# The last loads of a softmax over row dot products: eleven transfers in place of nine, the last one half a row

## The chip, the cores and the metric

The kernel runs on one core of a Trainium2 chip. The metric is the device time of one launch in microseconds (us): 320.58 us is the median of three runs of the kernel before, from 320.44 to 320.85 us.

## What is computed

Inputs x and y have 8 batches of 4096 rows of 512 float32 numbers. Only the diagonal of the product x·yᵀ is needed, that is one dot product of row n of x with row n of y, and then a softmax over the 4096 dots of each batch.

```
gram = np.matmul(x, y.transpose(0, 2, 1))
diag = np.diagonal(gram, axis1=1, axis2=2)
diag = diag - diag.max(axis=-1, keepdims=True)
exp = np.exp(diag)
return (exp / exp.sum(axis=-1, keepdims=True)).astype(np.float32)
```

The inputs are 134.2 MB and the output 0.13 MB. Each number is read once, multiplied once and added once.

## The kernel before

**Tiling.** The 8 batches are two sets of four. Within a set the 128 partitions hold 4 batches by 32 stretches of 128 rows, so each partition owns 128 rows of a set. They are taken in steps of R = 32 rows; two sets of four steps make eight steps, t = 0 to 7. A step of x, or of y, is a block of 128 partitions by 16384 float32 numbers, 8.39 MB. x goes by turns into two tiles, `xs0` (even t) and `xs1` (odd t); y always into the one tile `ys`. Dot r of a step lands in a column of `diag0` (first set) or `diag1` (second set).

**Order.** The schedule is written out by hand: each engine runs its instructions in the order of the text. All loads and the stores of the first set are issued by the queue of SyncE (SP); the final store is issued by ScalarE.

**Steps 0 to 5** (lines 124 to 135): VectorE multiplies x by y in place (line 72, in two instructions, the second from a copy `side` that ScalarE makes of the last 6 rows of y, so that `ys` is free sooner), then sums each row (line 75); ScalarE sums two rows (line 80). The load of the next y waits until VectorE and ScalarE have read the tile `ys`.

**Step 6** (lines 137 to 147) does the same with ScalarE summing 30 rows.

**Step 7, the last** (lines 150 to 162), comes in nine transfers: x 15 rows, y 17, x 8, y 10, x 6, y 3, x 2, y 2, x 1. After each transfer `dots` (line 82) issues, for every row of which both halves are there, one fused instruction on VectorE (line 85): product and sum over 512 numbers, the sum going to the row's column of `diag1`. The first y transfer reuses the part of `ys` that step 6 has read first, and the second (y 10) waits for the last product of step 6.

**Completion semaphores.** SP's transfers use eight completion semaphores by turns, so the transfer that takes a semaphore again is issued only once the transfer eight places earlier has landed. In step 7 the x 15 rows have number 6, y 17 number 7, x 8 number 0, y 10 number 1, and so on to x 1 with number 6.

**The stores of the first set** (lines 167 and 168) stand in SP's text behind all loads: eight pieces of 16 partitions, each 8 KB. They take the semaphores from number 7 on: the second waits for x 8, the third for y 10, and the eighth for x 1, the last load.

**The end** (lines 169 and 170): the row maxima of the last 16 dots and of two maxima taken before (`mxp`, line 99), the maximum over the 32 partitions of a batch (`nmx`, line 93), the exponentials with their sum on ScalarE (line 106), the sum over the partitions (`sum`), the reciprocal (`rc`), the scaling (line 113), and the store from ScalarE (line 170). Each of these waits for the one before.

**Addresses.** In each partition `xs0` begins at byte 16512, `xs1` at 82048 and `ys` at 147584; each of the three is 128 bytes past a multiple of 512.

Of the kernel before, what the change touches and what calls it, by code (L numbers as in the profile page):

```python
# [1 line left out]

# [5 lines left out]


@with_exitstack
def kernel(
    ctx: ExitStack,
    tc: tile.TileContext,
    x: bass.AP,
    y: bass.AP,
    out: bass.AP,
):
    nc = tc.nc
    ctx.enter_context(tc.manual_schedule())  # L20
    f32 = mybir.dt.float32
    Alu = mybir.AluOpType
    Act = mybir.ActivationFunctionType
    X = mybir.AxisListType.X
    B, N, D = x.shape
    P = nc.NUM_PARTITIONS
    G = 32
    Q = P // G
    C = N // G
    R = 32  # L30
    H = R // 2
    K = 6
    W = 2
    F = H + 1
    L = 9
    S = B // Q * (C // R)


    xv = x.rearrange("(s b) (j c) d -> s (b j) c d", b=Q, j=G)
    yv = y.rearrange("(s b) (j c) d -> s (b j) c d", b=Q, j=G)  # L40
    ov = out.rearrange("(s b) (j c) -> s (b j) c", b=Q, j=G)

    big = ctx.enter_context(tc.tile_pool(name="big", bufs=1))
    small = ctx.enter_context(tc.tile_pool(name="small", bufs=1))


    xs = [big.tile([P, R, D], f32, name=f"xs{i}") for i in range(2)]
    ys = big.tile([P, R, D], f32, name="ys")
    side = big.tile([P, K, D], f32, name="side")

    diag = [small.tile([P, C + 2 * i], f32, name=f"diag{i}") for i in range(B // Q)]
    res = [small.tile([P, C], f32, name=f"res{i}") for i in range(B // Q)]

    def columns(t, r0, n):
        c0 = t % (C // R) * R + r0
        return slice(c0, c0 + n)

    def rows(t, r0, n):
        return xs[t % 2][:, r0 : r0 + n, :]

    def dots_of(t, r0, n):
        return diag[t * R // C][:, columns(t, r0, n)]

    def load_x(t, r0, n):
        nc.sync.dma_start(out=rows(t, r0, n), in_=xv[t * R // C, :, columns(t, r0, n), :])  # L65

    def load_y(t, r0, n):
        nc.sync.dma_start(out=ys[:, r0 : r0 + n, :], in_=yv[t * R // C, :, columns(t, r0, n), :])  # L68

    def products(t, r0, n, yt):  # L70
        xt = rows(t, r0, n)
        nc.vector.tensor_tensor(out=xt, in0=xt, in1=yt, op=Alu.mult)  # L72

    def sums(t, r0, n):
        nc.vector.tensor_reduce(out=dots_of(t, r0, n), in_=rows(t, r0, n), axis=X, op=Alu.add)  # L75

    def sums_act(t, r0, n):
        for r in range(r0, r0 + n):
            row = xs[t % 2][:, r, :]
            nc.scalar.activation(out=row, in_=row, func=Act.Copy, accum_out=dots_of(t, r, 1))  # L80

    def dots(t, r0, n):
        for r in range(r0, r0 + n):
            xt = xs[t % 2][:, r, :]
            nc.vector.scalar_tensor_tensor(  # L85
                out=xt, in0=xt, scalar=1.0, in1=ys[:, r, :], op0=Alu.mult, op1=Alu.mult,
                accum_out=dots_of(t, r, 1),
            )

    def over_quadrant(name, column, op, negate=False):  # L90

        got = small.tile([P, 1], f32, name=name)
        nc.vector.tensor_reduce(  # L93
            out=got, in_=column.to_broadcast([P, G]), axis=X, op=op, negate=negate, apply_transpose=True
        )
        return got

    def largest(out, d):
        nc.vector.tensor_reduce(out=out, in_=d, axis=X, op=Alu.max)  # L99

    def exps(i, d):
        mxp = small.tile([P, 1], f32, name=f"mxp{i}")
        largest(mxp, d)
        nmx = over_quadrant(f"nmx{i}", mxp, Alu.max, negate=True)
        sump = small.tile([P, 1], f32, name=f"sump{i}")
        nc.scalar.activation(out=res[i], in_=diag[i][:, :C], func=Act.Exp, bias=nmx, scale=1.0, accum_out=sump)  # L106
        return sump

    def normalize(i, sump):
        total = over_quadrant(f"sum{i}", sump, Alu.add)  # L110
        rc = small.tile([P, 1], f32, name=f"rc{i}")
        nc.vector.reciprocal(out=rc, in_=total)  # L112
        nc.vector.tensor_single_scalar(out=res[i], in_=res[i], scalar=rc, op=Alu.mult)  # L113

    nc.scalar.preload_act_table(Act.Exp)  # L117
    nc.vector.addr_align(128, offset=0, max_nops=0)
    nc.scalar.addr_align(128, offset=0, max_nops=0)

    nc.sync.drain()  # L121
    nc.sync.drain()  # L122

    for t in range(S - 2):
        load_x(t, 0, R)
        load_y(t, 0, R)
        nc.scalar.activation(out=side, in_=ys[:, R - K :, :], func=Act.Copy)  # L127
        if t == C // R:
            normalize(0, sump)
        products(t, 0, R - K, ys[:, : R - K, :])  # L130
        products(t, R - K, K, side)
        sums(t, 0, R - W)
        sums_act(t, R - W, W)
        if t == C // R - 1:
            sump = exps(0, diag[0])

    t = S - 2
    load_x(t, 0, R)
    load_y(t, 0, R)
    spare = rows(t + 1, R - L, L)  # L140
    nc.scalar.activation(out=spare, in_=ys[:, F - L : F, :], func=Act.Copy)  # L141
    products(t, 0, F - L, ys[:, : F - L, :])
    products(t, F - L, L, spare)
    products(t, F, R - F, ys[:, F:, :])
    sums(t, R - W, W)
    sums_act(t, 0, R - W)
    largest(diag[1][:, C + 1 :], diag[1][:, : C - 2 * R])


    t += 1  # L150
    upto = {load_x: 0, load_y: 0}
    done = 0
    for load, n in (
        (load_x, H - 1), (load_y, F), (load_x, 8), (load_y, 10), (load_x, 6), (load_y, 3), (load_x, 2), (load_y, 2), (load_x, 1)
    ):
        load(t, upto[load], n)
        upto[load] += n
        both = min(upto.values())
        dots(t, done, both - done)
        done = both  # L160
        if done == F:
            largest(diag[1][:, C : C + 1], diag[1][:, C - 2 * R : C - R + H])

    met = small.tile([P, C - R], f32, name="met")
    nc.scalar.activation(out=met, in_=diag[1][:, : C - R], func=Act.Copy)  # L165

    for p in range(0, P, H):
        nc.sync.dma_start(out=ov[0, p : p + H, :], in_=res[0][p : p + H, :])
    normalize(1, exps(1, diag[1][:, C - R + H :]))
    nc.scalar.dma_start(out=ov[1], in_=res[1])  # L170


# [1 line left out]
_INS = ['x', 'y']  # L174
_OUTS = [((8, 4096), 'float32')]


# [23 lines left out]
```

## Time and profile before

| | |
|---|---|
| median of three runs | 320.58 us (320.44 to 320.85) |
| span of the profiled execution, first to last instruction | 318.6 us |
| around that span (median less span) | about 2.0 us |
| read from memory | 134.22 MB, 422 GB/s over the span |
| VectorE busy | 241.6 us, 76% |
| ScalarE busy | 49.8 us, 16% |

The page of the profile gives, for one execution, the busy time of each engine (DVE is VectorE, ACT ScalarE, POOL GpSimd, SP SyncE), the share of the DMA engines in 40 slices, the chain of work that ended last, the costliest groups of instructions, and the DMA issues with the time from issue to landing. Finer views give that chain and the instructions in order of time: start, duration, engine, line, operation. A name such as SPq or DVEq is the engine's instruction queue. A transfer's landing is its issue time plus its time to landing; several transfers in one queue overlap, so a time to landing of 19 us is mostly waiting behind earlier bytes. No time of its own is listed for the profiled execution beyond the span.

### The profile page before, as it was taken

Reading aid. Unit: us, or ns where it says so; the run is one execution under the profiler, and the core shown is the slowest. Engines: PE = TensorE matmul, PEld = TensorE weight load, DVE = VectorE, ACT = ScalarE, POOL = GpSimd, SP = SyncE. Lnnn points to the kernel's source line nnn. Section 1 sums busy time; section 2 is a strip of 40 time slices with the busy share of each in tenths; the row PEclk is TensorE's granted clock in tenths of the full one; section 3 lists DMA queues with packets and bytes.
Section 4 is the critical chain, followed back from the end, with each engine's and each line's share of the span. In section 5 each row is a group of like instructions: output and inputs, shape, how many; then the busy total and the mean of one; then the engine's idle time right before and its main releaser. Section 6 shows DMA issues by size and latency. Waiting matters only on the chain.

```text
span 318.6 us, 315 instructions
## 1 busy us (share of the span) xinstructions
DVE 241.6 (76%) x98; ACT 49.8 (16%) x97; POOL 0.2 (0%) x4
## 2 busy tenths in 40 slices
DVE  0000069995899939999399994999939998599996
ACT  1000030100301003010120103001030100596700
POOL 0000000000000000000000000000000000000000
DMA  9999999999999999999999999999999999999993
GB/s 389 403 395 486 436 395 436 486 395 395 494 428 395 469 453 395 395 510 411 395 477 444 395 444 477 395 395 494 428 395 469 453 395 403 432 443 413 427 411 120
DMA packets 3714, 134.37 MB, mean 422 GB/s; under 512 B 512, under 2 KB 768, under 8 KB 1280
## 3 DMA queue, kind: packets, MB, share of 16 engines
q1 hardware_dynamic: 3568, 134.29, 97.8%
q10 hardware_dynamic: 144, 0.07, 0.1%
q14 instruction: 2, 0.02, 0.0%
HBM read 134.22 MB, written 0.13 MB: 422 GB/s over the span
## 4 chain that ended last, share of the span: by engine, by line
DMA 65%; DVE 33%; SPq 1%; issue 0%; ACT 0%; DVEq 0%
DMA ys<-in_y_dram 65%; DVE xs L72 32%; DVE xs L85 0%; SPq L65 0%; SPq L68 0%; DVE res L113 0%; DVE sum L93 0%; DVE nmx L93 0%; ACT res L106 0%; DVE mxp L99 0%; DVE rc L112 0%; DVEq L72 0%; SPq L122 0%; SPq L121 0%
## 5 line engine op out<-in xcount | busy, mean ns | idle before, releaser
L72 DVE TENSOR_TENSOR xs<-xs,ys 128x13312 f32<-128x13312 f32 (+2 forms) x8 | 96.7, 12091 | 71.7 <-DMA ys<-in_y_dram 71.7
L75 DVE TENSOR_REDUCE diag<-xs 128x30 f32<-128x15360 f32 (+1 forms) x7 | 98.1, 14019 | 0.2
L80 ACT ACTIVATE xs<-xs 128x512 f32<-128x512 f32 x42 | 25.9, 617 | 90.4 <-DVE xs L72 90.4
L127 ACT ACTIVATE side<-ys 128x3072 f32<-128x3072 f32 x6 | 16.6, 2763 | 124.3 <-DMA ys<-in_y_dram 124.3
L85 DVE SCALAR_TENSOR_TENSOR xs<-xs,ys 128x512 f32<-128x512 f32 x32 | 19.9, 686 | 1.1 <-DMA ys<-in_y_dram 1.0
L72 DVE TENSOR_TENSOR xs<-xs,side 128x3072 f32<-128x3072 f32 x6 | 20.1, 3350 | 0.0
L80 ACT ACTIVATION_READ_ACCUMULATOR xs<-xs 128x1 f32 x42 | 7.9, 187 | 0.0
L141 ACT ACTIVATE xs<-ys 128x4608 f32<-128x4608 f32 x1 | 4.0, 4043 | 20.0 <-DMA ys<-in_y_dram 20.0
L106 ACT ACTIVATE res<-diag,nmx 128x128 f32<-128x128 f32 x2 | 0.8, 401 | 30.1 <-DVE nmx L93 30.1
L72 DVE TENSOR_TENSOR xs<-xs,xs 128x4608 f32<-128x4608 f32 x1 | 5.0, 4951 | 0.0
L85 DVE DVE_READ_ACCUMULATOR xs<-xs,ys 128x1 f32 x32 | 2.6, 81 | 0.0
L117 ACT ACT_TABLE_LOAD x1 | 1.3, 1283 | 0.7 <-PEq L185 0.7
L93 DVE TRANSPOSE_TENSOR_REDUCE sum<-sump 128x1 f32<-128x32 f32 x2 | 0.4, 211 | 1.2 <-ACT res L106 1.2
L113 DVE TENSOR_SCALAR res<-res,rc 128x128 f32<-128x128 f32 x2 | 0.6, 286 | 0.1
L99 DVE TENSOR_REDUCE mxp<-diag 128x1 f32<-128x128 f32 (+1 forms) x2 | 0.5, 228 | 0.1
L93 DVE TRANSPOSE_TENSOR_REDUCE nmx<-mxp 128x1 f32<-128x32 f32 x2 | 0.4, 211 | 0.1
L99 DVE TENSOR_REDUCE diag<-diag 128x1 f32<-128x64 f32 (+1 forms) x2 | 0.4, 202 | 0.0
L112 DVE RECIPROCAL rc<-sum 128x1 f32<-128x1 f32 x2 | 0.3, 164 | 0.1
L106 ACT ACTIVATION_READ_ACCUMULATOR res<-diag,nmx 128x1 f32 x2 | 0.4, 186 | 0.0
L165 ACT ACTIVATE met<-diag 128x96 f32<-128x96 f32 x1 | 0.3, 282 | 0.0
L185 POOL MEMSET const-bfloat16-1.0<- 128x1 bf16 x1 | 0.1, 101 | 0.0
L185 POOL MEMSET const-uint8-127<- 128x1 uint8 x1 | 0.1, 101 | 0.0
(2 smaller groups left out, 0.2 us busy)
## 6 DMA issues: line engine op xcount, KB each, us to landing
ys<-in_y_dram SPq DMA_DIRECT2D x1, 4352.0 KB, 14.8
xs<-in_x_dram SPq DMA_DIRECT2D x1, 3840.0 KB, 14.2
ys<-in_y_dram SPq DMA_DIRECT2D x1, 2560.0 KB, 12.9
xs<-in_x_dram SPq DMA_DIRECT2D x1, 2048.0 KB, 19.4
xs<-in_x_dram SPq DMA_DIRECT2D x1, 1536.0 KB, 16.2
ys<-in_y_dram SPq DMA_DIRECT2D x1, 768.0 KB, 17.7
xs<-in_x_dram SPq DMA_DIRECT2D x1, 512.0 KB, 18.5
ys<-in_y_dram SPq DMA_DIRECT2D x1, 512.0 KB, 19.3
```

Source lines behind the costliest of these rows:

```text
L72: nc.vector.tensor_tensor(out=xt, in0=xt, in1=yt, op=Alu.mult)
L75: nc.vector.tensor_reduce(out=dots_of(t, r0, n), in_=rows(t, r0, n), axis=X, op=Alu.add)
L80: nc.scalar.activation(out=row, in_=row, func=Act.Copy, accum_out=dots_of(t, r, 1))
L85: nc.vector.scalar_tensor_tensor(out=xt, in0=xt, scalar=1.0, in1=ys[:, r, :], op0=Alu.mult, op1=Alu.mult, accum_out=dots_of(t, r, 1),)
L93: nc.vector.tensor_reduce(out=got, in_=column.to_broadcast([P, G]), axis=X, op=op, negate=negate, apply_transpose=True)
L99: nc.vector.tensor_reduce(out=out, in_=d, axis=X, op=Alu.max)
L106: nc.scalar.activation(out=res[i], in_=diag[i][:, :C], func=Act.Exp, bias=nmx, scale=1.0, accum_out=sump)
L112: nc.vector.reciprocal(out=rc, in_=total)
L113: nc.vector.tensor_single_scalar(out=res[i], in_=res[i], scalar=rc, op=Alu.mult)
L117: nc.scalar.preload_act_table(Act.Exp)
L127: nc.scalar.activation(out=side, in_=ys[:, R - K :, :], func=Act.Copy)
L141: nc.scalar.activation(out=spare, in_=ys[:, F - L : F, :], func=Act.Copy)
```

## The change

```
+    E = 16
+    V = D // 2
...
-    xs = [big.tile([P, R, D], f32, name=f"xs{i}") for i in range(2)]
-    ys = big.tile([P, R, D], f32, name="ys")
+    xflat = [big.tile([P, R * D + E], f32, name=f"xs{i}") for i in range(2)]
+    yflat = big.tile([P, R * D + E], f32, name="ys")
+    xs = [t[:, : R * D].rearrange("p (r d) -> p r d", d=D) for t in xflat]
+    ys = yflat[:, : R * D].rearrange("p (r d) -> p r d", d=D)
...
+    def dot(xt, yt, out):
+        nc.vector.scalar_tensor_tensor(
+            out=xt, in0=xt, scalar=1.0, in1=yt, op0=Alu.mult, op1=Alu.mult, accum_out=out
+        )
...
+    nc.gpsimd.memset(yflat[:, R * D :], 1.0)
+    chained = xflat[t % 2][:, R * D : R * D + 1]
+    late = R * D - V
...
-        (load_x, H - 1), (load_y, F), (load_x, 8), (load_y, 10), (load_x, 6), (load_y, 3), (load_x, 2), (load_y, 2), (load_x, 1)
+        (load_x, H - 1), (load_y, F), (load_x, 8), (load_y, 9), (load_x, 6), (load_y, 3), (load_y, 1)
...
+    first = (R - 3) * D
+    xt = xflat[t % 2]
+    xrow = xv[t * R // C].rearrange("p c d -> p (c d)")
+    end = ((t % (C // R)) + 1) * R * D
+    nc.sync.dma_start(out=xt[:, first : late], in_=xrow[:, end - R * D + first : end - V])
+    dots(t, done, 1)
+    load_y(t, R - 2, 1)
+    dots(t, R - 2, 1)
+    load_y(t, R - 1, 1)
+    dot(xt[:, late - V : late], yflat[:, late - V : late], chained)
+    nc.sync.dma_start(out=xt[:, late : R * D], in_=xrow[:, end - V : end])
+    dot(xt[:, late : R * D + 1], yflat[:, late : R * D + 1], dots_of(t, R - 1, 1))
...
-    for p in range(0, P, H):
-        nc.sync.dma_start(out=ov[0, p : p + H, :], in_=res[0][p : p + H, :])
+    for p, n in ((0, H), (H, H), (2 * H, H), (3 * H, H), (4 * H, 2 * H), (6 * H, 2 * H)):
+        nc.sync.dma_start(out=ov[0, p : p + n, :], in_=res[0][p : p + n, :])
```

The last step comes in eleven transfers: x 15 rows, y 17, x 8, y 9, x 6, y 3, y 1 (row 29), x 2½ (rows 29, 30 and the first half of 31), y 1 (row 30), y 1 (row 31), x ½. The bytes are the same.

Row 31 becomes two instructions. The first multiplies and sums 256 numbers and puts its sum into a spare column behind the last row of the x tile. The second runs over the other 256 numbers and that column, whose partner in the y tile is a 1 that GpSimd has written once, so its sum over 257 numbers is the whole dot.

Each of the three large tiles has 16 more columns (64 bytes). `xs0` stays at byte 16512, `xs1` moves to 82112 (192 bytes past a multiple of 512) and `ys` to 147712 (256 bytes past one).

The first set is stored in six pieces, four of 16 partitions and two of 32. By the semaphores taken in turn, y 1 (row 31) is issued after y 17 has landed, x ½ after x 8 has landed, and the six stores after y 9, x 6, y 3, the y of row 29, x 2½ and the y of row 30 have landed. No store waits for the last load.

The dot of row 29 waits for two transfers; the second half of row 31 waits for its x, for the sum of the first half, and for GpSimd.

6 lines of the change are left out of this document (1 added, 5 removed).

## The prediction

> **What bounds the kernel now.** I read the page's totals and its chain of waits first.
>
> ```profile
> span 318.6 us, 315 instructions
> ...
> DVE 241.6 (76%) x98; ACT 49.8 (16%) x97; POOL 0.2 (0%) x4
> ...
> DMA  9999999999999999999999999999999999999993
> ...
> DMA ys<-in_y_dram 65%; DVE xs L72 32%; DVE xs L85 0%; SPq L65 0%; SPq L68 0%; DVE res L113 0%; DVE sum L93 0%; DVE nmx L93 0%; ACT res L106 0%; DVE mxp L99 0%; DVE rc L112 0%; DVEq L72 0%; SPq L122 0%; SPq L121 0%
> ```
>
> The DMA engines are full in every slice but the last; no engine is. The 32% that the chain gives to VectorE's products are waits of the next y load, during which the x load already in the queue keeps the DMA full, so they are not a second bound. That is checked in the same chain in order of time (start, length, what):
>
> ```profile
> 42.28 0.03 issue
> 42.31 0.02 DVEq L72
> 42.33 0.05 issue
> 42.38 14.04 DVE xs L72
> ...
> 56.49 24.49 DMA ys<-in_y_dram
> ...
> 249.97 24.52 DMA ys<-in_y_dram
> ...
> 293.76 19.28 DMA ys<-in_y_dram
> 313.04 0.02 issue
> 313.06 1.36 DVE xs L85 x4
> ```
>
> The y of step 1 lands at 56.49 + 24.49 = 80.98, that of step 6 at 249.97 + 24.52 = 274.49. Between them lie five steps of two blocks, 10 x 8.39 = 83.9 MB in 193.51 us: 433.5 GB/s without a gap, or 0.605 us for one row of 128 partitions (262144 bytes). So the end is set by when the last bytes land and by what follows them. The bytes are unchanged, and only the last 10 us can move, unless the rate itself does.
>
> **The end before.** The loads of step 7 by issue (SP's instructions in time) and by time to landing (the page's DMA issues):
>
> ```profile
> 279.45 0.43 SPq L65 DMA_DIRECT2D xs<-in_x_dram  x1
> 291.97 0.33 SPq L68 DMA_DIRECT2D ys<-in_y_dram  x1
> 292.34 0.43 SPq L65 DMA_DIRECT2D xs<-in_x_dram  x1
> 292.81 0.43 SPq L68 DMA_DIRECT2D ys<-in_y_dram  x1
> 293.29 0.43 SPq L65 DMA_DIRECT2D xs<-in_x_dram  x1
> ```
> ```profile
> ys<-in_y_dram SPq DMA_DIRECT2D x1, 2560.0 KB, 12.9
> xs<-in_x_dram SPq DMA_DIRECT2D x1, 2048.0 KB, 19.4
> xs<-in_x_dram SPq DMA_DIRECT2D x1, 1536.0 KB, 16.2
> ys<-in_y_dram SPq DMA_DIRECT2D x1, 768.0 KB, 17.7
> xs<-in_x_dram SPq DMA_DIRECT2D x1, 512.0 KB, 18.5
> ...
> out_dram<-res SPq DMA_DIRECT2D x8, 8.0 KB, 5.0
> ...
> out_dram<-res ACTq DMA_DIRECT2D x1, 64.0 KB, 1.6
> ```
>
> VectorE in time, where a DVE_READ_ACCUMULATOR after each dot writes its sum:
>
> ```profile
> 304.43 0.20 DVE L99 TENSOR_REDUCE diag<-diag 128x1 f32<-128x48 f32 x1
> 304.93 0.69 DVE L85 SCALAR_TENSOR_TENSOR xs<-xs,ys 128x512 f32<-128x512 f32 x1 [0.31 <-DMA ys<-in_y_dram]
> ...
> 312.29 0.69 DVE L85 SCALAR_TENSOR_TENSOR xs<-xs,ys 128x512 f32<-128x512 f32 x1
> 312.90 0.08 DVE L85 DVE_READ_ACCUMULATOR xs<-xs,ys 128x1 f32 x1
> 313.06 0.69 DVE L85 SCALAR_TENSOR_TENSOR xs<-xs,ys 128x512 f32<-128x512 f32 x1
> 313.68 0.08 DVE L85 DVE_READ_ACCUMULATOR xs<-xs,ys 128x1 f32 x1
> 313.71 0.69 DVE L85 SCALAR_TENSOR_TENSOR xs<-xs,ys 128x512 f32<-128x512 f32 x1
> 314.33 0.08 DVE L85 DVE_READ_ACCUMULATOR xs<-xs,ys 128x1 f32 x1
> 314.44 0.17 DVE L99 TENSOR_REDUCE mxp<-diag 128x1 f32<-128x18 f32 x1
> ...
> 316.19 0.37 ACTq L170 DMA_DIRECT2D out_dram<-res  x1
> ```
>
> Landings: y 10 at 304.91 (its dot starts 0.02 later, as at 313.04 in the chain), x 6 at 292.34 + 16.2 = 308.54, y 3 at 310.51, x 2 at 311.79, y 2 at 313.04, and x 1 at 313.69, since row 31 starts at 313.71, a little later than VectorE alone would allow. VectorE runs rows 17 to 29 back to back: from 304.93 to 312.90, 13 dots at 0.613 us. So it and the transfers end together, and a gain needs both to move. From the last landing to `mxp` it takes 0.75 us; from `mxp` on (the rest of the softmax and the final store, 316.19 + 1.6 = 317.8) nothing changes.
>
> **The change, part by part.** *Two more transfers.* Gaps between the landings less the bytes' time at 433.5 GB/s: x 6 0.00, y 3 0.16, x 2 0.07, y 2 0.04, x 1 0.04 us. The new transfers are nearest to the last three: I take 0.05 us each, with bounds of 0 and 0.16. From y 10's landing less one row, y 9 lands at 304.31, x 6 (3.63 later) at 307.94, y 3 (1.97) at 309.91, then y 29 at 310.57, x 2½ at 312.13, y 30 at 312.78, y 31 at 313.44, x ½ at 313.79: 0.10 later than the last load before.
>
> In a sentence by itself: the Trainium skill ("SBUF — State Buffer", The DMA setup-cost knee) gives every transfer a roughly fixed 2 us, by which two more would put the kernel at about 324.6. The landings 1.25 and 0.65 us apart contradict it for transfers that queue behind others.
>
> *SP's queue.* x ½ is issued only when x 8 has landed, 279.45 + 19.4 = 298.85, with six stores behind it. That is some 14 us ahead of its bytes' turn, with seven transfers still queued in front; it costs nothing while that cover lasts. Its own 0.43 us and that of one other issue are hidden the same way. The six stores stand behind all loads in the queue; the last is now released at 312.78 instead of 313.69 and lands before the final store is even issued at 316.19, as the eight did. Nothing is gained there.
>
> *The memset* is one GpSimd instruction that waits for nothing and ends in the first 42 us, before VectorE's first product: nothing. Without cover it would cost about 0.1 us (the four small ones of before make 0.2 us busy, rounded on the page).
>
> *Row 31 in halves.*
>
> ```profile
> L72 DVE TENSOR_TENSOR xs<-xs,ys 128x13312 f32<-128x13312 f32 x6 | 84.2, 14026 | 66.5 <-DMA ys<-in_y_dram 66.5
> L85 DVE SCALAR_TENSOR_TENSOR xs<-xs,ys 128x512 f32<-128x512 f32 x32 | 19.9, 686 | 1.1 <-DMA ys<-in_y_dram 1.0
> L72 DVE TENSOR_TENSOR xs<-xs,ys 128x4096 f32<-128x4096 f32 x1 | 4.4, 4426 | 5.2 <-DMA ys<-in_y_dram 5.2
> ```
>
> (14026 − 4426)/9216 = 1.042 ns for each further number, so 512 cost 0.533 us of the 0.613 us cadence and a half dot takes 0.346 us to its accumulator read, which adds 0.08. The new wait: the second half reads the sum of the first. The cheap end for that is 0.03 us, from the read at 314.33 + 0.08 to `mxp` at 314.44; the dear end 0.10, because the instruction waits for several things at once, as the first product did (42.28 to 42.38). I take 0.10, the form it is nearest to, also for row 29, which now waits for two transfers. Queued behind the waiting instruction is `mxp` and, through it, everything to the end.
>
> *Sum.* Rows 17 to 28, twelve dots, start after line 99's maximum at 304.65 instead of 304.93 and end at 312.01; VectorE is 0.28 us ahead and no longer what is late. Row 29 starts at 312.13 + 0.10 = 312.23, row 30 at 312.84 (its y has been there since 312.78), the first half at 313.46, its sum is written at 313.89, the second half starts at 313.99 (x ½ has been there since 313.79), and `mxp` at 313.99 + 0.346 + 0.08 + 0.03 = 314.45. Before it was 314.44. What the shorter last dot saves, 0.27 us, the wait between the halves and the two transfers take back. So +0.01 on a span of 318.6; with the 2.0 us around it that is **320.6** beside the median 320.58. With no price for a transfer and 0.02 and 0.03 for the waits, the same walk ends at 314.19 (−0.25); with 0.16 for each short transfer, at 314.90 (+0.46): 320.3 to 321.05.
>
> **Rivals.** *(a) The y tile's new place makes its loads faster.* `ys` now starts 256 bytes past a multiple of 512, not 128. If the price per transfer is really one per row and engine, 0.06 us (the mean of the five gaps) for 8 of the 128 rows on each of 16 engines, that is 7.5 ns; if it came from the odd start and fell away for y, 7 whole and 6 partial y transfers of 8 rows would save 104 x 7.5 ns = 0.78 us: **319.8**. For: the loads set the time everywhere. Against: it must come from the start and not from the row's own handling, and no row separates these.
>
> The Trainium skill ("DMA: Bandwidth & Descriptors", How a descriptor splits into AXI transactions) says that a run not starting at a multiple of 256 bytes is cut once more; one piece in 257 of y's 155 us would be an estimate of 0.60 us. It states this of descriptors in general, and nothing here shows it for the SBUF side.
>
> *(b) `xs1`, at 192 instead of 128, loads slower.* Three whole and five partial x transfers are 64 rows per engine; at 7.5 ns 0.48 us, at the 20 ns of y 3's gap 1.28: 321.1 to **321.9**. It decides from 10 ns a row on. For: same as (a). Against: 128 was not a round place either, and ran without visible loss.
>
> *(c) The short transfers at the end pay a completion time that does not overlap.* The final store, alone in its queue, took 1.6 us for 64 KB, whose bytes need 0.15; two times 1.45 would be +2.9: **323.5**. It ends slower than the bound from 0.32 us each on. Against: x 1 landed 0.65 us after y 2.
>
> *(d) The walk is right but the DVE's dots do not start earlier*, because y 9 lands later than 304.65: then rows 17 to 28 slip, and from 0.2 us of slip on row 29 does; up to 320.9, inside the forecast's own range.
>
> **How the numbers follow.** A difference of 0.2%, 0.64 us, is about what a measurement of this kernel can tell from no change. My forecast, with (d), has 0.70: its whole range lies within that bound. (a) has 0.15 and is the faster case; (b) 0.09 and (c) 0.06 make the slower 0.15. The range runs from (a)'s 319.8 to 321.2, above the forecast's upper end by the runs' own spread; what lies beyond is half of (a), most of (b) and (c), under 0.2.
>
> **What would show it.** Right: the y landings of whole steps stay 38.70 us apart; the last x lands at 313.7 to 313.9; the second half starts about 0.1 us after the first half's accumulator read, not at its own x's landing; `mxp` stays within 0.3 us of 314.44. (a) or (b): y-to-y 38.6 or 38.8 us, a difference that grows from step to step. (c): gaps of over 0.9 us between single rows at the end. I am wrong if `mxp` moves by more than 0.5 us.

## The result and the profile after

The changed kernel takes 320.1 us (median of 21 runs, 319.63 to 320.64), the kernel before in the same series 320.5 us (320.33 to 320.93). The ratio is 0.9986, 95% interval 0.998 to 0.9991: faster by 0.14%, some 0.45 us (0.40 us by the two medians). That is less than the 0.2% of the forecast's chances, but clear of zero, and the forecast said no change (320.6). The profiled execution of the changed kernel took 319.84 us with a span of 318.1.

First SP's instructions in time, of the changed kernel: the y loads of steps 1 and 6, the first and second y load of step 7, x 2½ and the half row.

```profile
56.48 0.33 SPq L72 DMA_DIRECT2D ys<-in_y_dram  x1
...
249.69 0.33 SPq L72 DMA_DIRECT2D ys<-in_y_dram  x1
...
278.74 0.33 SPq L72 DMA_DIRECT2D ys<-in_y_dram  x1
...
291.64 0.33 SPq L72 DMA_DIRECT2D ys<-in_y_dram  x1
...
293.44 0.43 SPq L176 DMA_DIRECT2D xs<-in_x_dram  x1
...
298.46 0.33 SPq L182 DMA_DIRECT2D xs<-in_x_dram  x1
```

The step from one y load to the next is (249.69 − 56.48)/5 = 38.64 us; before it was (249.97 − 56.49)/5 = 38.70. The difference grows with every step, in a part of the kernel of which no instruction was changed: at the second y load of step 7 it is 0.33 us (291.64 against 291.97). Only after that point do the two texts differ. There the page's DMA issues (KB, us to landing) and VectorE in time say:

```profile
ys<-in_y_dram SPq DMA_DIRECT2D x1, 2304.0 KB, 12.2
...
xs<-in_x_dram SPq DMA_DIRECT2D x1, 640.0 KB, 18.2
xs<-in_x_dram SPq DMA_DIRECT2D x1, 128.0 KB, 14.7
```
```profile
304.05 0.20 DVE L104 TENSOR_REDUCE diag<-diag 128x1 f32<-128x48 f32 x1
304.16 0.68 DVE L87 SCALAR_TENSOR_TENSOR xs<-xs,ys 128x512 f32<-128x512 f32 x1
...
310.89 0.69 DVE L87 SCALAR_TENSOR_TENSOR xs<-xs,ys 128x512 f32<-128x512 f32 x1
311.50 0.08 DVE L87 DVE_READ_ACCUMULATOR xs<-xs,ys 128x1 f32 x1
311.70 0.69 DVE L87 SCALAR_TENSOR_TENSOR xs<-xs,ys 128x512 f32<-128x512 f32 x1
312.32 0.08 DVE L87 DVE_READ_ACCUMULATOR xs<-xs,ys 128x1 f32 x1
312.32 0.69 DVE L87 SCALAR_TENSOR_TENSOR xs<-xs,ys 128x512 f32<-128x512 f32 x1
312.93 0.09 DVE L87 DVE_READ_ACCUMULATOR xs<-xs,ys 128x1 f32 x1
312.93 0.42 DVE L87 SCALAR_TENSOR_TENSOR xs<-xs,ys 128x256 f32<-128x256 f32 x1
313.27 0.08 DVE L87 DVE_READ_ACCUMULATOR xs<-xs,ys 128x1 f32 x1
313.45 0.43 DVE L87 SCALAR_TENSOR_TENSOR xs<-xs,ys 128x257 f32<-128x257 f32 x1
313.80 0.08 DVE L87 DVE_READ_ACCUMULATOR xs<-xs,ys 128x1 f32 x1
313.92 0.17 DVE L104 TENSOR_REDUCE mxp<-diag 128x1 f32<-128x18 f32 x1
```

Row 29 (311.70) waits for x 2½, which lands at 293.44 + 18.2 = 311.64; from there VectorE is busy without a gap to the wait between the halves: the sum of the first half is written at 313.27 + 0.08 = 313.35, the last half row of x has been there since 298.46 + 14.7 = 313.16, and the second half starts at 313.45. `mxp` starts at 313.92 instead of 314.44. Of these 0.52 us, 0.33 were there before the changed transfers began. From the second y load's issue to `mxp` it is 22.28 us, against 314.44 − 291.97 = 22.47 before.

### The profile page after: what moved, and what is told of

It is laid out like the page before. It is cut to its first block, busy times and chain, and to the rows that moved or that the text cites. A ratio compares the mean times of both kernels' runs of the same rounds, so it can differ in the third digit from the quotient of the medians.

```text
span 318.1 us, 320 instructions
## 1 busy us (share of the span) xinstructions
DVE 241.6 (76%) x100; ACT 49.8 (16%) x97; POOL 0.3 (0%) x5
## 5 line engine op out<-in xcount | busy, mean ns | idle before, releaser
L87 DVE SCALAR_TENSOR_TENSOR xs<-xs,ys 128x512 f32<-128x512 f32 (+2 forms) x33 | 20.0, 673 | 0.8 <-DMA ys<-in_y_dram 0.6
## 6 DMA issues: line engine op xcount, KB each, us to landing
ys<-in_y_dram SPq DMA_DIRECT2D x1, 2304.0 KB, 12.2
xs<-in_x_dram SPq DMA_DIRECT2D x1, 640.0 KB, 18.2
```

Of the source, the lines that this page charges most:

```text
L87: nc.vector.scalar_tensor_tensor(out=xt, in0=xt, scalar=1.0, in1=yt, op0=Alu.mult, op1=Alu.mult, accum_out=out)
```

## Experiments

Theories: **P**, the place of the tiles: `ys` (or the x tiles) starting at another remainder makes every load into it faster; **T**, the tail: the new order of the last transfers gains, and the whole steps differ only from execution to execution. Each kernel was timed beside the kernel before on the same chip. Unused tiles in the diffs only shift what stands behind them.

### The places without the tail, and the tail without the places

p1, the kernel before with the longer tiles alone:

```
-    xs = [big.tile([P, R, D], f32, name=f"xs{i}") for i in range(2)]
-    ys = big.tile([P, R, D], f32, name="ys")
+    xflat = [big.tile([P, R * D + E], f32, name=f"xs{i}") for i in range(2)]
+    yflat = big.tile([P, R * D + E], f32, name="ys")
```

> The kernel before with the three large tiles 64 bytes longer, as in the change, and nothing else: xs1 starts 192 and ys 256 bytes past a multiple of 512; transfers, dots and stores are those of before. Theory P (the place of the y tile makes its loads faster): two neighbouring whole y issues stand 38.65 us apart as in the changed kernel (38.70 before), the second y load of the last step (y 10) is issued at about 291.64 (291.97 before), mxp starts about 314.0, time 320.1. Theory T (the whole steps differ only from execution to execution, the gain is the order of the last transfers): 38.70 apart, y 10 at 291.97, time 320.5.

Measured: 320.01 us, before 320.35; ratio 0.9989 (0.998 to 0.9997).

p2, the changed kernel with the old remainders:

```
-    E = 16
+    E = 128
...
-    xflat = [big.tile([P, R * D + E], f32, name=f"xs{i}") for i in range(2)]
+    xflat = [big.tile([P, R * D + i * E], f32, name=f"xs{i}") for i in range(2)]
```

> The changed kernel with the spare columns made so that xs0, xs1 and ys all start 128 bytes past a multiple of 512, as before (no spare columns in xs0, 128 in xs1 and in ys). Theory P: whole y issues 38.70 us apart, y 9 issued at 291.97, and of the gain only the tail's is left: mxp at about 314.25, time 320.3. Theory T: time 320.1, as the changed kernel.

Measured: 320.46 us, before 320.35; ratio 1.0011 (1.0 to 1.0022). The 320.3 that theory P left to the tail is not there.

So the places alone give the gain, and the eleven transfers with the halved row give none: T falls. The pitch that was expected, 38.65 or 38.70 us, neither profiled execution shows: single steps of p1's took up to 39.06 us and of p2's up to 39.05 (the last section has more of such steps), and p1's execution was the longest of its eleven (320.43 us). Where p1 was to issue its second y load of step 7 at 291.64, it did so at 292.22. The pitch is read from r4 and p4, below. How long the tail itself is, in the same measure as above (the second y load of step 7 to `mxp`), does show in p1 and p2, as the difference of two rows. SP and VectorE in time, p1:

```profile
292.22 0.33 SPq L71 DMA_DIRECT2D ys<-in_y_dram  x1
```
```profile
314.51 0.17 DVE L102 TENSOR_REDUCE mxp<-diag 128x1 f32<-128x18 f32 x1
```

The same two rows of p2:

```profile
292.43 0.33 SPq L72 DMA_DIRECT2D ys<-in_y_dram  x1
```
```profile
315.00 0.17 DVE L104 TENSOR_REDUCE mxp<-diag 128x1 f32<-128x18 f32 x1
```

| second y load of step 7 to `mxp`, us | old places | new places |
|---|---|---|
| nine transfers | 22.47 (before) | 22.29 (p1) |
| eleven, row 31 in halves | 22.57 (p2) | 22.28 (the change) |

Across: the places shorten the tail by 0.2 to 0.3 us. Down: the new transfers change it by −0.01 or +0.10 us. Each entry is one execution.

### Which places

p3 and p4 put unused columns in front of all three tiles of the kernel before, r4 moves only the x tiles:

```
+    big.tile([P, 96], f32, name="front")   # p3; 16 columns in p4
...
+    big.tile([P, 96], f32, name="front")   # r4
     xs = [big.tile([P, R, D], f32, name=f"xs{i}") for i in range(2)]
+    big.tile([P, 32], f32, name="gap")     # r4
     ys = big.tile([P, R, D], f32, name="ys")
```

> The kernel before with 384 unused bytes in front of xs0, so that xs0, xs1 and ys all start at a multiple of 512; nothing else. Theory P: the loads of x gain what those of y gained, about 0.05 us a step more: 38.60 apart, time 319.75. Theory T: 38.70 apart, 320.5.

> The kernel before with 64 unused bytes in front of xs0, so that all three tiles start 192 bytes past a multiple of 512, the place that xs1 has in the changed kernel. Theory P, if only a start at a multiple of 256 helps: 38.70 apart, 320.5, as before; if a start off a multiple of 128 costs more, over 38.75 apart and above 320.8. Theory T: 320.5.

> The kernel before, loads uncut, with xs0 and xs1 at multiples of 512 and ys still 128 bytes past one. If, as with the cut loads, either tensor's place gives most of the gain, 0.999 of before, 0.35 us faster; if only y's place counts with whole blocks, 1.000.

| | start of the tiles, bytes past a multiple of 512 | us (before) | ratio |
|---|---|---|---|
| p4 | all 192 | 320.45 (320.35) | 1.0004 (0.9995 to 1.0013) |
| p1 | xs0 128, xs1 192, ys 256 | 320.01 (320.35) | 0.9989 (0.998 to 0.9997) |
| p3 | all 0 | 320.03 (320.35) | 0.9988 (0.9979 to 0.9996) |
| r4 | xs0 and xs1 0, ys 128 | 319.91 (320.37) | 0.9987 (0.9979 to 0.9996) |

192 is as good as 128, so rival (b) of the prediction is not there. Moving y helps, moving x helps as much, and both together not more: p3's expectation missed. The profiles of p4 and r4 show the pitch; none of their instructions was changed. The y loads of steps 1 and 6 in p4:

```profile
56.42 0.33 SPq L69 DMA_DIRECT2D ys<-in_y_dram  x1
...
249.91 0.33 SPq L69 DMA_DIRECT2D ys<-in_y_dram  x1
```

and in r4, with its second y load of step 7 and its `mxp`:

```profile
56.45 0.33 SPq L70 DMA_DIRECT2D ys<-in_y_dram  x1
...
249.67 0.33 SPq L70 DMA_DIRECT2D ys<-in_y_dram  x1
...
291.62 0.33 SPq L70 DMA_DIRECT2D ys<-in_y_dram  x1
```
```profile
313.83 0.17 DVE L101 TENSOR_REDUCE mxp<-diag 128x1 f32<-128x18 f32 x1
```

A step of p4 takes (249.91 − 56.42)/5 = 38.70 us, as before; one of r4 (249.67 − 56.45)/5 = 38.64, as in the changed kernel, and r4's tail of 22.21 us is as short as the change's. So the whole gain shows without one of the new transfers. With all three tiles at multiples of 512 it shows less cleanly: in p3 and in r1 (below) the steps alternate between about 38.6 and 38.7 us, 38.67 and 38.66 on average, and the tail is as long as before (22.46 and 22.51). Why, no run shows.

The effects are near what eleven runs can resolve, so the next kernels enlarge it.

### The same in four times as many pieces

Every whole-step load is cut into 4 transfers of 8 rows, so each partition's piece, its contiguous run of bytes in one transfer, is 16 KB and there are four times as many pieces; then the tiles are moved by unused columns as above.

```
-        load_x(t, 0, R)
-        load_y(t, 0, R)
+        for r in range(0, R, 8):
+            load_x(t, r, 8)
+        for r in range(0, R, 8):
+            load_y(t, r, 8)
```

> The kernel before with each whole-step load (steps 0 to 6, x and y) cut into 4 transfers of 8 rows, so each partition's piece is 16 KB instead of 64 KB and there are four times as many; tiles where they were (128 bytes past a multiple of 512). A baseline for the next three. If each short piece of a partition costs 6 to 7.5 ns on its DMA engine whatever its start, 2 x 7 x 24 more of them per engine cost +2.0 to +2.5 us: 322.5 to 323. If pieces cost nothing, 320.4.

> The cut loads, with 384 unused bytes between xs1 and ys, so that ys alone starts at a multiple of 512. Theory P1 (every piece that starts off a multiple of 256 costs a fixed bit more, x and y alike; from the 0.34 us of the run with the places alone over 56 whole and some 30 partial pieces per engine about 4 ns): 256 pieces of y per engine save about 1.0 us against the cut baseline. Theory P2 (only the place of y counts, per piece): the same 1.0 us. Theory P3 (the place changes the rate of bytes, not the cost of a piece): 0.35 us.

> The cut loads, with xs0 and xs1 at multiples of 512 and ys 128 bytes past one. P1: about 1.0 us less than the cut baseline. P2: no difference from it. P3: 0 to 0.35 us less.

> The cut loads, with all three tiles at multiples of 512. P1: about 2.0 us less than the cut baseline. P2: about 1.0 us less. P3: 0.35 us less.

> The cut loads (4 transfers of 8 rows a block) with ys alone moved, to 256 bytes past a multiple of 512, its place in the changed kernel; xs0 and xs1 stay at 128. If any multiple of 256 is a good start: 1.007 of before, as with ys at a multiple of 512 (1.9 us less than the cut baseline's 1.0131). If a multiple of 512 is needed: 1.0131; then the changed kernel's gain has another cause than y's start.

> The cut loads with all three tiles at 192 bytes past a multiple of 512. If every start off a multiple of 256 costs the same: 1.0131, as the cut baseline at 128. If the cost grows with the distance from 256 or for odd multiples of 64: over 1.015.

> The cut loads with ys alone moved, to 288 bytes past a multiple of 512, 32 past a multiple of 256; xs0 and xs1 at 128. If what counts is a start at a multiple of 256: 1.0131, as the cut baseline. If what counts is only that ys and xs do not share the same remainder by 256: 1.007, as with ys at 256.

The chains of waits, in order of time, give the products of steps 1 and 5, which start when y has landed: four whole steps apart. q1 (no tile moved), q2 (y at a multiple of 512), q4 (all three):

```profile
82.12 14.04 DVE xs L72
...
238.74 14.04 DVE xs L72
```
```profile
81.31 14.04 DVE xs L73
...
237.08 14.04 DVE xs L73
```
```profile
81.44 14.04 DVE xs L73
...
237.04 14.04 DVE xs L73
```

and s1, with y 256 past a multiple of 512 (the other steps of the table are read in the same way):

```profile
81.43 14.04 DVE xs L73
...
237.19 14.04 DVE xs L73
```

| | xs, ys past a multiple of 512 | one step, us | us | ratio |
|---|---|---|---|---|
| q1 | 128, 128 | 39.16 | 324.54 | 1.0131 (1.0117 to 1.0145) |
| s2 | 192, 192 | 39.16 | 324.49 | 1.0131 (1.0115 to 1.0146) |
| s3 | 128, 288 | 39.19 | 324.58 | 1.0132 (1.0115 to 1.0149) |
| s1 | 128, 256 | 38.94 | 322.71 | 1.0076 (1.0061 to 1.0091) |
| q2 | 128, 0 | 38.94 | 322.62 | 1.007 (1.0057 to 1.0082) |
| q3 | 0, 128 | 38.94 | 322.81 | 1.0074 (1.006 to 1.0087) |
| q4 | 0, 0 | 38.90 | 322.3 | 1.006 (1.0047 to 1.0073) |

The effect is now 1.7 to 2.2 us and the intervals are apart. A tile that starts at a multiple of 256 loads faster; 256 does as well as 512, while 128, 192 and 288 are all alike. s3 rules out that a mere difference between x and y is what counts. VectorE's product takes 14.03 or 14.04 us in all of them, so it is the loads that changed and not the engine that reads the tiles. With y moved a step saves 0.21 us (39.155 − 38.943), over 4 x 8 pieces of y per DMA engine: 6.6 ns for each. Uncut it was 38.70 − 38.64, more exactly 0.054 us over 8 pieces: 6.7 ns. The price is one per piece, not one per byte (P3 falls).

Two expectations missed in size. P1 and P2 gave 1.0 us to a moved y and it was 1.9, because their 4 ns a piece came from p1's 0.34 us alone. And cutting alone (q1) cost 4.2 us where 2.0 to 2.5 were expected: 39.16 − 38.70 = 0.46 us a step, or 9.6 ns for each of the 48 more pieces per engine, makes 3.2 of it; most of the other 1.0 us falls after step 5.

The Trainium skill ("DMA: Bandwidth & Descriptors", How a descriptor splits into AXI transactions) has the boundary: a run that does not start at a multiple of 256 bytes is cut once more. The table agrees on 256, here for the side of a load that is written, while the page's wording is of reads. By the page's count a 16 KB piece becomes 65 parts instead of 64, an estimate of 0.30 us for one block of 39.16/2 = 19.58 us; with y moved, a step became 0.21 us shorter.

x and y do not add: moving both saves 0.26 us a step, not 0.42 (P1 and P2 both miss). Where that comes from can be read in the kept traces, which also list every DMA packet with its bytes and its length; 128 packets of one size are one transfer, a packet for each partition's piece. Mean length in ns for four transfers of step 7, whose text is the same in these kernels:

| transfer, bytes of a packet | before (x 128, ys 128) | p4 (192, 192) | p1 (128 and 192, 256) | r4 (0, 128) | p3 (0, 0) |
|---|---|---|---|---|---|
| y 17, 34816 | 1292.0 | 1292.5 | 1288.0 | 1288.0 | 1288.0 |
| y 10, 20480 | 765.2 | 765.9 | 761.0 | 761.1 | 761.0 |
| x 6, 12288 | 463.7 | 463.7 | 460.0 | 460.0 | 460.0 |
| y 3, 6144 | 237.1 | 237.1 | 234.0 | 234.0 | 234.0 |

A piece costs 3 to 5 ns more at any of these sizes while both streams are off a multiple of 256. One stream moved takes that from the pieces of both: in p1 x 6 gains although `xs1` stays off, in r4 y 17 gains although `ys` stays off. So the 6.6 ns are about half y's own and half x's. The 16 KB pieces of the cut loads say the same (steps 2 to 5): 614.4 to 614.7 ns in q1 for x and for y, in q2 611.2 for the moved y and 612.0 for the unmoved x, in q3 611.1 for x and 612.1 for y, in q4 611.0 for both. What stays **open** is why one stream at a good start relieves the other.

### The rest of the change, piece by piece

r2, the changed kernel with row 31 whole:

```
-    nc.sync.dma_start(out=xt[:, first : late], in_=xrow[:, end - R * D + first : end - V])
+    load_x(t, R - 3, 2)
...
-    dot(xt[:, late - V : late], yflat[:, late - V : late], chained)
-    nc.sync.dma_start(out=xt[:, late : R * D], in_=xrow[:, end - V : end])
-    dot(xt[:, late : R * D + 1], yflat[:, late : R * D + 1], dots_of(t, R - 1, 1))
+    load_x(t, R - 1, 1)
+    dots(t, R - 1, 1)
```

> The changed kernel, places and all, with row 31 as one whole dot: x 2 rows (29, 30) in place of 2 1/2 and x 1 row last in place of half a row, still eleven transfers. The walk of the prediction, fed with the changed kernel's landings: row 29 starts 0.2 us sooner, row 31 with the last landing at about 313.2, mxp at 313.93 against 313.92: no difference, 0.9986 of before. If the half row is what gained: 0.4 us slower, 0.9999 of before.

Measured: 319.9 us, before 320.37; ratio 0.9989 (0.998 to 0.9997). VectorE in time, at the end of r2:

```profile
312.08 0.69 DVE L87 SCALAR_TENSOR_TENSOR xs<-xs,ys 128x512 f32<-128x512 f32 x1
312.70 0.08 DVE L87 DVE_READ_ACCUMULATOR xs<-xs,ys 128x1 f32 x1
313.18 0.69 DVE L87 SCALAR_TENSOR_TENSOR xs<-xs,ys 128x512 f32<-128x512 f32 x1 [0.39 <-DMA xs<-in_x_dram]
313.79 0.08 DVE L87 DVE_READ_ACCUMULATOR xs<-xs,ys 128x1 f32 x1
313.91 0.17 DVE L104 TENSOR_REDUCE mxp<-diag 128x1 f32<-128x18 f32 x1
```

The whole row waits 0.39 us for its x, and `mxp` still starts at 313.91, against 313.92 with the halves. The half row buys an earlier start and pays it back in the wait between its halves.

r3, the changed kernel with eight stores of the first set:

```
-    for p, n in ((0, H), (H, H), (2 * H, H), (3 * H, H), (4 * H, 2 * H), (6 * H, 2 * H)):
-        nc.sync.dma_start(out=ov[0, p : p + n, :], in_=res[0][p : p + n, :])
+    for p in range(0, P, H):
+        nc.sync.dma_start(out=ov[0, p : p + H, :], in_=res[0][p : p + H, :])
```

> The changed kernel with the first set stored in eight pieces of 16 partitions again, the last two released by the y of row 31 and by the last load. Stores land by about 315.5, the final store is issued at 315.7: no difference from the changed kernel, 0.9986 of before. If the released stores held up the end: 0.2 us or more slower.

Measured: 320.13 us, before 320.37; ratio 0.9991 (0.9982 to 1.0). Its interval covers the change's 0.9986, so a cost of the two late stores, if any, is under what was resolved.

r1, all three tiles of the changed kernel at multiples of 512 (96 unused columns in front, 128 spare ones in `xs1`, 16 in `ys`):

```
+    big.tile([P, 96], f32, name="front")
-    xflat = [big.tile([P, R * D + E], f32, name=f"xs{i}") for i in range(2)]
+    xflat = [big.tile([P, R * D + i * E], f32, name=f"xs{i}") for i in range(2)]
```

> The changed kernel with xs0, xs1 and ys all at multiples of 512 (384 unused bytes in front, 128 spare columns in xs1, 16 in ys), meant to beat both. From the kernel before with the same places (0.9988) and the cut loads (aligning x beside y saved 0.3 of 2.2 us at four times the pieces): if x's place adds a little, 0.997 to 0.9985 of before, 319.4 to 319.9; if y's place alone is all there is to have, 0.9986 as the change.

Measured: 320.05 us, before 320.37; ratio 0.9988 (0.998 to 0.9997): no better than the change. None of the uncut kernels with a tile at a multiple of 256 is faster than another beyond its interval; r4, the kernel before with its x tiles moved and not one other line changed, is among them.

## Why the prediction was right and wrong

**The step that failed** is the sentence "The bytes are unchanged, and only the last 10 us can move, unless the rate itself does". The rate did. The prediction held this as rival (a), "The y tile's new place makes its loads faster", and gave it 0.15, because no row of the profile before separated a price for an odd start from a price for every row. It was the mechanism of the gain: the sum lacked a term for the moved tiles, −0.33 us for the whole steps and −0.18 us in the tail (22.47 to 22.29, places alone).

**Its size.** Rival (a) took 7.5 ns a piece over 104 pieces and 0.78 us. By the steps it is 6.7 ns for each piece of y, but half of that came off the pieces of x, which the rival left out; the profiles of the change and of p1 give 0.33 + 0.18 = 0.51 us, the medians of the change and of p1 0.40 and 0.34. That 7.5 is so near 6.7 is luck: it was taken from the gaps of short transfers, in which nothing told an odd start from what every piece costs. The sign to look for was named rightly (a difference that grows from step to step).

**The walk through the tail** forecast +0.01 us. Measured by the table of four it is −0.01 to +0.10 us: right. Step by step: x 2½ was to land at 312.13 and landed at 311.64, of which 0.33 is the earlier start; from row 29's start to `mxp` it was to take 314.45 − 312.23 = 2.22 us and took 313.92 − 311.70 = 2.22. Row 29's wait for two transfers was to cost 0.10 and cost about 0.06 (311.64 to 311.70). The wait between the halves was to cost 0.10, the dear end: 313.35 to 313.45. The cadence of a half dot, 0.346: 312.93 to 313.27.

**The transfer's price** of 0.05 us made it 1.66 us from x 2½ to x ½, three transfers whose 655360 bytes take 1.51 at 433.5 GB/s. At the old places (p2: issues at 294.23 and 299.31, 18.4 and 15.0 us to landing) it was 314.31 − 312.63 = 1.68, at the new ones 313.16 − 311.64 = 1.52. Each landing is known to 0.05 us, so the price fits the old places and was too high for the new. Rival (c), a completion time that does not overlap, is not there, nor is (d): y 9 landed at 291.64 + 12.2 = 303.84, ahead of VectorE, which started on its rows at 304.16.

**What was costed at nothing** stayed so: the half row was issued at 298.46, 14.7 us before it landed; eight stores or six made no resolved difference.

## What to carry to other kernels

A change that adds a few bytes to a tile moves every tile behind it: before costing the edit itself, ask where the others now start. In a kernel bound by loads, start the loaded tiles at a multiple of 256 bytes; it costs some unused columns, and it matters the more, the shorter the contiguous run per partition (0.1% here with 64 KB, 0.5 to 0.7% with 16 KB). Where two streams load by turns, moving one gives most of the gain. And when a gain shows, compare the steps that were not edited first: a difference that grows there is not the edit's.

## What the runs showed that was not expected

**A start off 256 bytes costs 3 to 5 ns per contiguous piece** on its DMA engine, at 6 to 35 KB by the packets' lengths and at 16 and 64 KB by the steps, but only while both streams are off: one moved, x or y, takes most of it from the pieces of both.

**The cut itself costs too.** With all tiles at multiples of 512, a step takes 38.90 us in 16 KB pieces (q4) and 38.67 in 64 KB pieces (p3): 0.23 us over 48 more pieces per engine, about 5 ns each. A cut step also has six more transfers, and these two runs do not tell a price per piece from one per transfer.

**Single long steps.** In some executions one whole step takes some 0.4 us longer than the others, in kernels of either kind. SP in time, r3, the y loads of steps 3 to 6:

```profile
133.64 0.33 SPq L72 DMA_DIRECT2D ys<-in_y_dram  x1
...
172.35 0.33 SPq L72 DMA_DIRECT2D ys<-in_y_dram  x1
...
211.47 0.33 SPq L72 DMA_DIRECT2D ys<-in_y_dram  x1
...
250.16 0.33 SPq L72 DMA_DIRECT2D ys<-in_y_dram  x1
```

The steps are 38.71, 39.12 and 38.69 us. Such a step is as large as the whole effect; it is why one profile's span could not have told these kernels apart, while the regular pitch of the steps beside it could. Its cause stays open.
